# Sending 2 KB per partition of the pooled output on ScalarE's queue beside the loads (3-D average pooling)

## Chip, cores, metric

One Trainium2 chip, one of its cores. The metric is the device time of one execution in microseconds, as the median of several runs. A ratio is the mean time of one kernel's fast runs over the mean of the other's fast runs of the same rounds; it is therefore not quite the ratio of the medians quoted beside it.

## The reference

Average pooling with a 2 x 2 x 2 window over a float32 tensor of 8 x 32 x 32 x 32 x 32 (33.55 MB in, 4.19 MB out).

```python
window = x[:, :, d_s:d_s + 2, h_s:h_s + 2, w_s:w_s + 2]
result[:, :, i, j, k] = np.mean(window, axis=(-3, -2, -1))
```

## The kernel before

Batch and channels make 256 rows, two tiles of 128 partitions. A row has 32768 input values, loaded in units of up to 32 KB per partition (4 MB), five buffers deep, all on SyncE's queue. Per unit VectorE (DVE) adds planes, then neighbours in a row, then neighbouring rows with a scale of 1/8, into a buffer that holds the whole output of one tile (16 KB per partition).

```python
KF = 256
pool_in = ctx.enter_context(tc.tile_pool(name="pin", bufs=5))
obuf = [pool_out.tile([P, 16 * KF], F32, name=f"obuf{t}") for t in range(2)]

plan = [
    (0, 0, (32,)), (0, 32, (32,)), (0, 64, (32,)), (0, 96, (32,)),
    (1, 0, (32,)), (1, 32, (32,)), (1, 64, (16, 16)), (1, 96, (16, 16)),
]                                   # layout of the list changed here
# ... pool_unit: two nc.vector.tensor_add and one tensor_tensor_reduce ...

for t, k0, parts in plan:
    # ... one nc.sync.dma_start per part, then pool_unit per part ...

for t, k0, kb in [(0, 0, 16), (1, 0, 14), (1, 14, 2)]:
    nc.sync.dma_start(
        out=ov[t * P:(t + 1) * P, k0 * KF:(k0 + kb) * KF],
        in_=obuf[t][:, k0 * KF:(k0 + kb) * KF],
    )
# ... at the end of the program SyncE waits for the stores' semaphores ...
```

So there are three stores: the whole first output tile (16 KB per partition, 2 MB), 14 KB and then 2 KB per partition of the second. The 2 KB store covers the last pooled unit, the 14 KB store all of the second tile ahead of it.

Of the kernel before, what the change touches and what calls it, by code (L numbers as in the profile page):

```python
# [1 line left out]

# [4 lines left out]

F32 = mybir.dt.float32
KF = 256


@with_exitstack
def pool_rows(
    ctx: ExitStack,
    tc: tile.TileContext,
    x: bass.AP,
    kernel_size: int,
    out: bass.AP,
):
    nc = tc.nc  # L20
    assert kernel_size == 2, "only kernel_size == 2 supported"

    B, C, D, H, W = x.shape
    P = nc.NUM_PARTITIONS
    assert (B * C, D, H, W) == (2 * P, 32, 32, 32)
    add = mybir.AluOpType.add



    xv = x.rearrange("b c d h w -> (b c) (d h w)")  # L30
    ov = out.rearrange("b c d h w -> (b c) (d h w)")




    pool_in = ctx.enter_context(tc.tile_pool(name="pin", bufs=5))
    pool_out = ctx.enter_context(tc.tile_pool(name="pout", bufs=1))
    obuf = [pool_out.tile([P, 16 * KF], F32, name=f"obuf{t}") for t in range(2)]
    dummy = pool_out.tile([P, 1], F32, name="dummy")


    plan = [
        (0, 0, (32,)),
        (0, 32, (32,)),
        (0, 64, (32,)),
        (0, 96, (32,)),
        (1, 0, (32,)),
        (1, 32, (32,)),
        (1, 64, (16, 16)),
        (1, 96, (16, 16)),  # L50
    ]

    def pool_unit(buf, t, k0, kb):

        od = kb // 8
        a = buf.rearrange("p (o dd e) -> p o dd e", o=od, dd=2)
        b = buf[:, :od * 1024]
        nc.vector.tensor_add(  # L58
            out=b.rearrange("p (o e) -> p o e", o=od), in0=a[:, :, 0], in1=a[:, :, 1])
        bv = b.rearrange("p (e ww) -> p e ww", ww=2)  # L60
        c = buf[:, od * 1024:od * 1536]
        nc.vector.tensor_add(out=c, in0=bv[:, :, 0], in1=bv[:, :, 1])  # L62
        cv = c.rearrange("p (j hh k) -> p j hh k", hh=2, k=16)
        o0 = k0 * KF // 8
        nc.vector.tensor_tensor_reduce(  # L65
            out=obuf[t][:, o0:o0 + od * 256].rearrange("p (j k) -> p j k", k=16),
            in0=cv[:, :, 0], in1=cv[:, :, 1],
            scale=0.125, scalar=0.0, op0=add, op1=add, accum_out=dummy[:, :],
        )

    for t, k0, parts in plan:
        tin = pool_in.tile([P, 32 * KF], F32, tag="tin", name="tin")
        views = []
        o = 0
        for kb in parts:
            v = tin[:, o * KF:(o + kb) * KF]
            nc.sync.dma_start(
                out=v, in_=xv[t * P:(t + 1) * P, (k0 + o) * KF:(k0 + o + kb) * KF])
            views.append((v, k0 + o, kb))
            o += kb  # L80
        for v, k, kb in views:
            pool_unit(v, t, k, kb)


    for t, k0, kb in [(0, 0, 16), (1, 0, 14), (1, 14, 2)]:
        nc.sync.dma_start(
            out=ov[t * P:(t + 1) * P, k0 * KF:(k0 + kb) * KF],
            in_=obuf[t][:, k0 * KF:(k0 + kb) * KF],
        )


def kernel(tc: tile.TileContext, x: bass.AP, kernel_size: int, out: bass.AP):
    nc = tc.nc
    pool_rows(tc, x, kernel_size, out)
    tc.close()
    tc.compile()  # L96
    blocks = nc.main_func.blocks



    opening, program = blocks[0].instructions, blocks[tc.starting_block_idx].instructions
    load = next(i for i in program if isinstance(i, mybir.InstDMACopy))
    assert load.engine == nc.sync.engine
    barrier = next(
        n for n, i in enumerate(opening)
        if i.engine == load.engine and isinstance(i, mybir.InstDrain))
    program.remove(load)
    opening.insert(barrier, load)




    closing = blocks[-1].instructions
    stores = [
        i for i in program
        if isinstance(i, mybir.InstDMACopy) and "out_" in i.outs[0].memref]
    kept = [u.id for i in stores for u in i.sync_info.on_update]
    final = next(
        i for i in closing
        if i.engine == nc.sync.engine and isinstance(i, mybir.InstDrain))  # L120
    waits = {w.id: w for w in final.sync_info.on_wait}
    closing[closing.index(final)] = mybir.InstDrain(
        name=final.name, engine=final.engine, ins=[], outs=[], is_reset_sema=False,
        sync_info=mybir.SyncInfo(
            on_wait=[w for n, w in waits.items() if n not in kept], on_update=[]))


    reset = next(
        n for n, i in enumerate(closing)
        if isinstance(i, mybir.InstDrain) and i.is_reset_sema)  # L130
    first, stop = closing[reset].reset_range_start, closing[reset].reset_range_stop
    assert isinstance(closing[reset + 1], mybir.InstISA)
    while len(closing) > reset:
        closing.pop()
    n = first
    while n < stop:
        m = n
        while m < stop and m not in kept:
            m += 1
        if m > n:  # L140
            closing.append(mybir.InstDrain(
                name=nc.get_next_instruction_name(), engine=nc.gpsimd.engine, ins=[], outs=[],
                is_reset_sema=True, reset_range_start=n, reset_range_stop=m))
            nc.gpsimd.sem_clear(range(n, m))
        n = m + 1
    for n in kept:
        w = waits[n]
        closing.append(mybir.InstEventSemaphore(
            name=nc.get_next_instruction_name(), engine=nc.sync.engine, ins=[], outs=[],
            sync_info=mybir.SyncInfo(  # L150
                on_wait=[w],
                on_update=[mybir.SyncUpdate(
                    sync_type="semaphore", id=n, ant_name=w.ant_name,
                    update_mode="sem-sub-imm", update_value=w.wait_value)])))


# [1 line left out]
_INS = ['x', 'kernel_size']  # L158
_OUTS = [((8, 32, 16, 16, 16), 'float32')]

_NUMBERS = {'kernel_size': 2}


# [26 lines left out]
```

## Time and profile before

| | before |
|---|---|
| time, median of 3 (range) | 91.97 us (91.76 to 92.02) |
| span of the profile (first to last instruction that it counts) | 86.4 us |
| DVE busy | 64.0 us |
| share of the 16 DMA engines on SyncE's queue | 99.2% |
| last store issued, landed | 85.2 us, 90.6 us |

The span ends at DVE's last instruction, while the last stores are still under way: here the span is not the time. Most of the lines that carry the reading stand in the prediction; one more, from the timeline, is VectorE's start after its sixth load:

```profile
60.65 4.43 DVE L58 TENSOR_TENSOR tin<-tin 128x4096 f32<-128x4096 f32 x1 [1.70 <-DMA tin<-in_x_dram]
```

Each record of a DMA packet in the trace has a start, a duration and a size; where the text speaks of packet records, the numbers were worked out from those.

### The profile page before, as it was taken

What the parts mean: (1) busy time and instruction counts of PE and PEld (TensorE: products, weight loads), DVE (VectorE), ACT (ScalarE), POOL (GpSimd) and SP (SyncE); (2) the same over time, 40 slices, a digit from 0 to 9 for tenths busy, and PEclk for the clock granted to TensorE, in tenths of its full rate; (3) what the DMA queues carried; (4) which work ended last, traced back from release to release, by engine and by line L of the source; (5) the groups of instructions that cost most, each with busy time, mean ns of one, the idle gap of its engine ahead of it and who ended that gap; (6) DMA issues with size and microseconds to landing.
All of it is one profiled execution on the core that took longest, in us unless ns stands there. A gap on an engine that the chain in (4) does not pass through costs nothing.

```text
span 86.4 us, 90 instructions
## 1 busy us (share of the span) xinstructions
DVE 64.0 (74%) x40; POOL 0.2 (0%) x4
## 2 busy tenths in 40 slices
DVE  0000039993999749993999749992999999999994
POOL 0000000000000000000000000000000000000000
DMA  8979997999979999799979999799999999998999
GB/s 243 425 319 470 486 470 319 425 486 486 455 319 440 486 486 410 319 486 486 470 319 425 486 486 440 304 470 387 455 402 455 395 455 410 440 425 319 448 432 408
DMA packets 1634, 36.37 MB, mean 421 GB/s; under 512 B 176, under 2 KB 176, under 8 KB 176
## 3 DMA queue, kind: packets, MB, share of 16 engines
q1 hardware_dynamic: 1634, 36.37, 99.2%
HBM read 33.55 MB, written 4.19 MB: 437 GB/s over the span
## 4 chain that ended last, share of the span: by engine, by line
DMA 61%; DVE 37%; issue 0%; DVEq 0%
DMA tin<-in_x_dram 61%; DVE tin L58 21%; DVE tin L62 11%; DVE obuf L65 6%; DVE dummy L65 0%; DVEq L96 0%
## 5 line engine op out<-in xcount | busy, mean ns | idle before, releaser
L58 DVE TENSOR_TENSOR tin<-tin 128x4096 f32<-128x4096 f32 (+1 forms) x10 | 35.7, 3569 | 20.6 <-DMA tin<-in_x_dram 20.6
L62 DVE TENSOR_TENSOR tin<-tin 128x2048 f32<-128x2048 f32 (+1 forms) x10 | 18.6, 1864 | 0.3
L65 DVE CUSTOM_DVE_ANT_1 obuf<-tin 128x1024 f32<-128x1024 f32 (+1 forms) x10 | 10.1, 1011 | 0.3
L65 DVE DVE_READ_ACCUMULATOR2_ANT dummy<- 128x1 f32 x10 | 0.8, 82 | 0.0
L171 POOL MEMSET const-bfloat16-1.0<- 128x1 bf16 x1 | 0.1, 102 | 0.0
L171 POOL MEMSET const-uint8-127<- 128x1 uint8 x1 | 0.1, 101 | 0.0
L171 POOL MEMSET const-float32-1.0<- 128x1 f32 x1 | 0.1, 99 | 0.0
L171 POOL MEMSET const-float32-0.0<- 128x1 f32 x1 | 0.1, 98 | 0.2 <-issue 0.2
## 6 DMA issues: line engine op xcount, KB each, us to landing
tin<-in_x_dram SPq DMA_DIRECT2D x6, 4096.0 KB, 34.9
tin<-in_x_dram SPq DMA_DIRECT2D x4, 2048.0 KB, 38.0
out_dram<-obuf SPq DMA_DIRECT2D x1, 2048.0 KB, 36.4
out_dram<-obuf SPq DMA_DIRECT2D x1, 1792.0 KB, 9.1
out_dram<-obuf SPq DMA_DIRECT2D x1, 256.0 KB, 5.4
```

The costliest lines, as they stand in the source:

```text
L58: nc.vector.tensor_add(out=b.rearrange("p (o e) -> p o e", o=od), in0=a[:, :, 0], in1=a[:, :, 1])
L62: nc.vector.tensor_add(out=c, in0=bv[:, :, 0], in1=bv[:, :, 1])
L65: nc.vector.tensor_tensor_reduce(out=obuf[t][:, o0:o0 + od * 256].rearrange("p (j k) -> p j k", k=16), in0=cv[:, :, 0], in1=cv[:, :, 1], s ...
L171: nc = _bacc.Bacc("TRN2", target_bir_lowering=False, num_devices=1)
```

## The change

The intent, as far as the code shows it: part of the output should leave while the loads run, so that fewer bytes are left for the tail.

```diff
--- before
+++ after
-    for t, k0, kb in [(0, 0, 16), (1, 0, 14), (1, 14, 2)]:
-        nc.sync.dma_start(
+    for queue, t, k0, kb in [
+        (nc.scalar, 0, 0, 2),
+        (nc.sync, 0, 2, 14),
+        (nc.sync, 1, 0, 14),
+        (nc.sync, 1, 14, 2),
+    ]:
+        queue.dma_start(
             out=ov[t * P:(t + 1) * P, k0 * KF:(k0 + kb) * KF],
             in_=obuf[t][:, k0 * KF:(k0 + kb) * KF],
         )
@@
     kept = [u.id for i in stores for u in i.sync_info.on_update]
+    kept = [n for j, n in enumerate(kept) if n not in kept[j + 1:]]
```

The second part keeps one entry per semaphore in the end-of-program list, since two stores may now share one.

## The prediction

> **What bounds the kernel now**
>
> I read the page first (the slices, the queue, the chain), then the windows view by stage, the list of DMA issues, the waits of both engines, and the timeline of the tail.
>
> ```profile
> span 86.4 us, 90 instructions
> ...
> DMA  8979997999979999799979999799999999998999
> ...
> q1 hardware_dynamic: 1634, 36.37, 99.2%
> HBM read 33.55 MB, written 4.19 MB: 437 GB/s over the span
> ...
> DMA 61%; DVE 37%; issue 0%; DVEq 0%
> ```
>
> The reader is to see that one queue (q1, SyncE's) holds all 16 DMA engines for 99.2% of the span. The chain of waits says DMA 61% and DVE 37%, which looks like two bounds in turn. It isn't quite: the chain ends at the last instruction that counts as busy, and the last stores come after it.
>
> The row of slices seems to have holes (the sevens, and GB/s figures of 319). I take them for a counting effect: the trace's packet records show the 16 engines in step, each with one 32 KB packet of 1.213 us (median) after another, so that a short slice catches one more or one fewer start. Put into one chain per engine by their starts and ends, the records leave no gap above 0.11 us from the first packet to the last. Longer windows are flat:
>
> ```profile
> core 0: us, DVE busy (x) POOL busy (x), PEclk, DMA share, GB/s
> 0.00:12.10 12.10, 0.00 (x0) 0.20 (x4) 1.00 0.95 390
> 12.10:60.60 48.50, 39.75 (x20) 0.00 (x0) 1.00 1.00 430
> 60.60:81.00 20.40, 20.14 (x17) 0.00 (x0) 1.00 1.00 415
> 81.00:85.20 4.20, 4.13 (x6) 0.00 (x0) 1.00 1.00 426
> 85.20:90.60 5.40, 0.01 (x1) 0.00 (x0) 1.00 0.83 351
> ```
>
> The DMA share column is 1.00 from 12.1 us to 85.2 us, and 0.83 in the last stretch only because the transfers end inside it. DVE is full only from 60.6 us on. So what sets the end is bytes through the engines: 33.55 + 4.19 = 37.74 MB at 430 GB/s is 87.8 us, and the rest is start-up.
>
> ```profile
> out_dram<-obuf SPq DMA_DIRECT2D x1, 2048.0 KB, 36.4
> out_dram<-obuf SPq DMA_DIRECT2D x1, 1792.0 KB, 9.1
> out_dram<-obuf SPq DMA_DIRECT2D x1, 256.0 KB, 5.4
> ```
>
> The last column is time from issue to landing. A 256 KB store would need 0.61 us at 430 GB/s, yet takes 5.4: it stands in line behind other bytes. The 2 MB store is issued at 49.3 us and lands 36.4 us later, at 85.7: on the same queue as the loads it waits until all of them are through.
>
> ```profile
> 80.93 2.28 DVE L58 TENSOR_TENSOR tin<-tin 128x2048 f32<-128x2048 f32 x1
> 83.25 1.22 DVE L62 TENSOR_TENSOR tin<-tin 128x1024 f32<-128x1024 f32 x1
> 84.50 0.69 DVE L65 CUSTOM_DVE_ANT_1 obuf<-tin 128x512 f32<-128x512 f32 x1
> 85.12 0.08 DVE L65 DVE_READ_ACCUMULATOR2_ANT dummy<- 128x1 f32 x1
> ```
>
> The last unit is pooled at 85.2 us, its store is issued there and lands at 85.2 + 5.4 = 90.6. By the packet records the engines still work on the 1792 KB store until 88.9 to 89.6 and reach the last store only then, so DVE could end some time later at no cost. The measured 91.97 is 1.4 us after that landing; I keep 1.4 as a constant.
>
> ```profile
> DVE tin L58 <- DMA tin<-in_x_dram: 20.6, 6, 12.1
> ```
>
> DVE's only waits are the first six loads. After the sixth, at 60.65, it never waits again.
>
> **What the Trainium skill says**
>
> All four are from its page "DMA: Bandwidth & Descriptors". Section "Issuing engines are not separate DMA queues": DMAs from ScalarE, SyncE and GpSimd run on the same 16 engines and interleave, and a second issuing engine saves issue time only. The trace has nothing to save there: a store's issue takes 0.33 to 0.35 us of SyncE, and SyncE is mostly idle. Section "Where 436 GB/s comes from": a ceiling of 435 GB/s for the 16 ports; the trace agrees, with 430 over 48.5 us. Section "Queues, rings and completion order": each DMA engine goes round robin, packet by packet, over the rings that have work. The kernel before has one ring with data, so its trace cannot show it. Section "Latency and other measured facts", row on HBM row pitch: copies between HBM tensors over the sync and scalar queues ran at 207 to 214 GB/s per direction at their best. I read that as loads and stores in flight together at some 428 GB/s in sum, that is neither a free second direction nor a heavy price for mixing. No trace here shows it yet.
>
> **The change part by part**
>
> 1. Removed: an eighth of the 2048 KB store (256 KB; 2 KB of 16 KB per partition). Each engine owns 8 partitions, so its eight 16 KB packets of 0.611 us become eight of 14 KB. The 1792 KB store already has that size: 0.535 us. Saved at the tail: 8 x (0.611 - 0.535) = 0.61 us per engine.
>
> 2. Added: one store on ScalarE's queue, eight 2 KB packets per engine. The last store has that shape now: 0.084 us each, and 0.009 us for the completion write. Sum 8 x 0.084 + 0.009 = 0.68 us per engine. ScalarE has no other work, so its issue costs nothing on the path. Its data are ready when the first unit is pooled, 20.1 us; the framework may add a wait on an older semaphore, but any moment in the load phase gives the same sum.
>
> 3. Balance on the engines: 0.68 - 0.61 = +0.07 us. No byte goes away, none moves into an idle gap, for there is none.
>
> 4. Moved: the loads. With one small packet between two load packets, the 256 KB are through some 8 x 1.3 = 10 us after they start, so from the fourth load on everything lands 0.68 us later. DVE follows, since it waits for the loads until 60.65: that start becomes 61.3, the 20 us of work behind it is unchanged, and the last unit ends at 85.2 + 0.68 = 85.9. The last load (landing at 80.8 by the records) comes at 81.5, when DVE gets to it at 81.7; still no wait.
>
> 5. Is the later DVE end hidden? The loads free the engines at about 80.7 instead of 80.0, the shorter first store runs to about 84.9, the 1792 KB store to about 89.0. The last store is issued at 85.9; the first load took 1.0 to 1.95 us from issue to its first packet on the various engines, so its packets are ready at 87.9 at the latest, 1 us before the first engine is free. Hidden, with 1 us in hand. The end stays put: 90.6 + 0.07 + 1.4 = 92.0 to 92.1.
>
> So the change exchanges tail time for load time one to one.
>
> **The rivals**
>
> A. The two directions overlap. If the limit is the SBUF write side, the store (which reads SBUF) could pass beside loads for nothing. Then 0.68 us vanishes from the load phase and 0.61 stays saved: 91.97 - 0.61 = about 91.4. For it: the loads' 27.0 GB/s per engine might be a port's rate, not an engine's. Against: stores have the same rate (16 KB in 0.611 us against 0.613 for a 16 KB load packet), and the skill's 207 to 214 per direction.
>
> B. Mixing directions costs. For it: all 16 engines slow down together between 77 and 79.5 us, where 16 KB packets take up to 1.18 us instead of 0.613, some 0.6 us lost per engine, shortly before the first store packet starts at 79.8 to 80.5. If that is the price of turning from loads to stores, eight small packets between loads may pay part of it several times: one more such loss makes 92.6, the full price eight times makes 4.8 us, about 97. Against: it is seen once, 1 to 2 us before the turn itself, so it may be something else, and single small packets need not stop the stream.
>
> C. DVE or the last store becomes the bound. If the early store delayed the loads by over 0.68 + 1 us, the last store's packets would come to idle engines, and further delay would count in full. This needs B first.
>
> D. The turn's loss at 77 us goes away because writes have already happened once: up to 0.6 us less, 91.4 as well. I have nothing for it beyond the position of that loss.
>
> **Range and chances**
>
> The main line gives 92.04. A or D, together some 22%, would give about 91.4; B in a mild form (15%) about 92.6. The weighted middle stays at 92.0, and the three runs before scatter from 91.76 to 92.02. I predict 92.0 us, with 91.3 to 92.7 to hold it 8 times in 10. Faster by over 2% needs 90.1 or less: even the whole moved store for nothing and the whole loss at 77 us removed give 91.97 - 0.61 - 0.6 = 90.8. So 0.02. Slower by over 2% needs 93.8, a strong form of B: 0.05. Within 2%: 0.93.
>
> **What would show it right or wrong**
>
> - In the list of DMA queues a second queue with 0.26 MB, the DMA share still 1.00 in the long windows: right. A share below 1 or a rate clearly under 430 between 20 and 35 us: B. A rate above 435 there: A.
> - The sixth load's wait ending at 61.3 (+0.68): step 4. At 60.65: A.
> - DVE's last instruction at 85.9, so that the span grows by 0.7 us while the measured time does not: steps 4 and 5. A reader of the span alone would call the kernel slower.
> - The time from issue to landing of the last store down from 5.4 to about 4.8, as it is issued later and lands at the same moment: step 5.
> - A time of 91.5 or less makes the one-to-one exchange wrong, one of 92.8 or more the price of mixing.

## The result, and the profile after

The changed kernel: 92.06 us, median of 6 (91.84 to 92.11), against 91.93 (91.76 to 92.09) for the kernel before. The ratio is 1.001, with a 95% interval of 0.9992 to 1.0028: the same time. The prediction's 92.0 holds.

The page of the changed kernel, its span and its queues (packets, MB, share of 16 engines' span):

```profile
span 86.9 us, 90 instructions
...
q1 hardware_dynamic: 1654, 36.39, 98.7%
q10 hardware_dynamic: 144, 0.26, 0.8%
HBM read 33.55 MB, written 4.19 MB: 434 GB/s over the span
```

The second queue is there, with the 0.26 MB, and it has taken its share from the first: 98.7 + 0.8 is 99.5%, where one queue had 99.2%. The bytes are the same. The span is 0.5 us longer although the time isn't, which the prediction had warned of.

The windows by stage, the same as of before:

```profile
core 0: us, DVE busy (x) POOL busy (x), PEclk, DMA share, GB/s
0.00:12.10 12.10, 0.01 (x1) 0.20 (x4) 1.00 0.96 390
12.10:60.60 48.50, 39.74 (x20) 0.00 (x0) 1.00 1.00 429
60.60:81.00 20.40, 19.56 (x15) 0.00 (x0) 1.00 1.00 419
81.00:85.20 4.20, 4.13 (x5) 0.00 (x0) 1.00 1.01 434
85.20:90.60 5.40, 0.60 (x2) 0.00 (x0) 1.00 0.81 341
```

DMA share and GB/s have hardly moved in the long stages (429 for 430, 419 for 415); in the two short ones at the end the rates are 434 for 426 and 341 for 351. What has moved is DVE: 0.60 us of its work now lies in the last stretch, where there was 0.01.

The list of DMA issues (the last number is us from issue to landing, a median where there are two), DVE's waits, and three lines of the timeline:

```profile
out_dram<-obuf SPq DMA_DIRECT2D x2, 1792.0 KB, 22.0
out_dram<-obuf ACTq DMA_DIRECT2D x1, 256.0 KB, 14.1
out_dram<-obuf SPq DMA_DIRECT2D x1, 256.0 KB, 4.6
```

```profile
DVE tin L58 <- DMA tin<-in_x_dram: 21.1, 6, 12.1
```

```profile
20.14 0.38 ACTq L92 DMA_DIRECT2D out_dram<-obuf  x1
...
61.23 4.43 DVE L58 TENSOR_TENSOR tin<-tin 128x4096 f32<-128x4096 f32 x1 [1.69 <-DMA tin<-in_x_dram]
...
85.72 0.08 DVE L65 DVE_READ_ACCUMULATOR2_ANT dummy<- 128x1 f32 x1
```

The early store is issued at 20.14 us, at once when the first unit is pooled. DVE waits 21.1 us for loads where it waited 20.6, its sixth load comes at 61.23 instead of 60.65, and its last instruction starts at 85.72 instead of 85.12. The last store is issued 0.6 us later (85.83 for 85.23) and needs 4.6 us where it needed 5.4: it waits less in line. By the packet records the early store's packets of 0.084 us stand between load packets of 1.213 us, 1.29 us from one to the next on an engine, from 23.5 to 32.6 us.

### The profile page after: what moved, and what is told of

It reads as the page before. It is cut to its first block, busy times and chain, and to the rows that moved or that the text cites. A ratio compares the mean times of both kernels' runs of the same rounds, so it can differ in the third digit from the quotient of the medians.

```text
span 86.9 us, 90 instructions
## 1 busy us (share of the span) xinstructions
DVE 64.0 (74%) x40; POOL 0.2 (0%) x4
## 3 DMA queue, kind: packets, MB, share of 16 engines
q1 hardware_dynamic: 1654, 36.39, 98.7%
## 4 chain that ended last, share of the span: by engine, by line
DMA 61%; DVE 37%; issue 0%; DVEq 0%
DMA tin<-in_x_dram 61%; DVE tin L58 20%; DVE tin L62 11%; DVE obuf L65 6%; DVE dummy L65 0%; DVEq L102 0%
## 5 line engine op out<-in xcount | busy, mean ns | idle before, releaser
L58 DVE TENSOR_TENSOR tin<-tin 128x4096 f32<-128x4096 f32 (+1 forms) x10 | 35.7, 3570 | 21.1 <-DMA tin<-in_x_dram 21.1
## 6 DMA issues: line engine op xcount, KB each, us to landing
out_dram<-obuf ACTq DMA_DIRECT2D x1, 256.0 KB, 14.1
```

The source lines that it names most:

```text
L58: nc.vector.tensor_add(out=b.rearrange("p (o e) -> p o e", o=od), in0=a[:, :, 0], in1=a[:, :, 1])
```

## The experiments

My theory: all 16 engines are busy from the first load to the last store, so time is bytes at a fixed rate, and a store that leaves earlier delays the loads by as much as it shortens the tail. This holds until DVE is so late that a last store comes to idle engines. Rivals: the two directions overlap (a gain), mixing costs (a loss), and the second queue or the cut costs what the early leaving gains. A side question was the stretch of slow packets at 77 to 79 us.

In the diffs below only the list of stores is shown. Runs 1, 4, 5, 10 and 11 are written as edits of the changed kernel or of one another, runs 2, 3, 6 and 7 as edits of the kernel before.

**1. The cut without the early leaving**

```diff
-        (nc.scalar, 0, 0, 2),
+        (nc.sync, 0, 0, 2),
```

> The same four stores as the change, all on SyncE's queue: the cut without the early leaving. One-to-one theory: the tail pays for the cut alone (8 packets of 0.611 us become 8 of 0.535 and 8 of 0.084, and one completion write): +0.07 us, about 92.0, ratio 1.001, as the change itself; DVE ends at 85.2 us again, span 86.4. Rival (the early leaving gained something that the cut cost, or the reverse): ratio differs from the change's 1.001 by more than 0.003.

Measured: 91.91 us (91.61 to 92.3), ratio 0.9989 (0.9966 to 1.0013). DVE's waits, and from the timeline its start after the sixth load:

```profile
DVE tin L58 <- DMA tin<-in_x_dram: 20.5, 6, 12.1
```

```profile
60.63 4.43 DVE L58 TENSOR_TENSOR tin<-tin 128x4096 f32<-128x4096 f32 x1 [1.69 <-DMA tin<-in_x_dram]
```

DVE is back where it was before (60.63 for 60.65, span 86.3), and the time is the same. So the later DVE of the changed kernel comes from the early leaving and not from the cut, and neither is worth anything that can be measured. The two ratios, 0.9989 here and 1.001 of the change, differ by 0.002, within the bound that was set.

**2 and 3. 1 MB more, beside the loads or behind them**

Both keep the stores of before and write half of the first output tile once more into a spare tensor.

```diff
+    spare = nc.dram_tensor("spare", (P, 8 * KF), F32, kind="Internal").ap()
+    nc.scalar.dma_start(out=spare[:, :], in_=obuf[0][:, :8 * KF])   # run 2
+    nc.sync.dma_start(out=spare[:, :], in_=obuf[0][:, :8 * KF])     # run 3
```

> The kernel before with 1 MB more (8 KB per partition, once more the output's first half of the first tile) stored by ScalarE's queue into a spare tensor beside the loads. One-to-one: 8 packets of about 0.306 us more per engine, +2.46 us, 94.4, ratio 1.027; DVE ends at about 87.6. Overlapping directions (rival A): +0 to 0.5, ratio under 1.006. Price for mixing (rival B): more than +3 us, ratio above 1.033, and more than the same bytes cost behind the loads.

> The same 1 MB more, on SyncE's queue behind the loads, so that no store is beside a load. All theories: +2.46 us, 94.4, ratio 1.027, DVE ends at 85.2 as before. The difference from the run with the extra store beside the loads is what mixing itself costs (one-to-one: 0, within 0.3 us).

Measured: 94.23 us (ratio 1.0241, 1.0223 to 1.0259) beside the loads, 94.35 us (1.0257, 1.0237 to 1.0277) behind them. The page's queues and DVE's waits of the run beside the loads, then the same two of the run behind them:

```profile
q1 hardware_dynamic: 1651, 36.61, 96.6%
q10 hardware_dynamic: 144, 1.05, 2.8%
```

```profile
DVE tin L58 <- DMA tin<-in_x_dram: 23.5, 6, 12.3
```

```profile
q1 hardware_dynamic: 1692, 36.37, 99.5%
```

```profile
DVE tin L58 <- DMA tin<-in_x_dram: 20.6, 6, 12.1
```

Beside the loads, the extra megabyte adds 2.9 us to DVE's waiting; behind them, nothing. The time grows by 2.2 us in the one case and 2.3 in the other. This decides between the theories: overlap would have made run 2 about 92, a price for mixing would have made it longer than run 3. In packets of 8 KB, a byte stored beside loads costs what a byte stored behind them costs, within the noise. This is an equality of sums: by the packet records run 2 has slow packets worth 0.49 us per engine beside the loads and 0.05 at the end, run 3 has 0.01 and 0.73 (the table under runs 8 to 10). Both times are a little below the 2.46 us expected.

**4, 5 and 11. How much can leave early?**

The whole, half, and three quarters of the first output tile go on ScalarE's queue in stores of 4 KB per partition, each when its unit is pooled.

```diff
-        (nc.scalar, 0, 0, 2),
-        (nc.sync, 0, 2, 14),
+        (nc.scalar, 0, 0, 4),
+        (nc.scalar, 0, 4, 4),
+        (nc.scalar, 0, 8, 4),      # runs 4 and 11
+        (nc.scalar, 0, 12, 4),     # run 4
+        (nc.sync, 0, 8, 8),        # run 5
+        (nc.sync, 0, 12, 4),       # run 11
```

> The whole first output tile (2 MB) leaves on ScalarE's queue in four stores of 4 KB per partition, each when its unit is pooled. If the early bytes were a gain (rivals A, D): under 91.5. If they are exchanged one to one and nothing else bound: 92.2 (32 packets of 0.16 us for 8 of 0.611). With the limit that I named (the hidden delay of DVE is 1 to 2 us, here it is 5): loads end 5 us later, DVE's last unit ends at about 90.1, its store's packets come to idle engines at 91 to 92, the engines stand still for about 2 us between loads and stores: 94.3, from 93.6 to 95, ratio about 1.026. The slow packets at 77 to 79 us, if they belong to the turn from loads to stores, move to about 82 to 84; if to a moment of the run, they stay.

> Half of the first output tile (1 MB, two stores of 4 KB per partition) leaves on ScalarE's queue, the other half behind the loads. One-to-one with the hidden limit: loads end about 2.5 us later, DVE's last unit at about 87.7, the 1792 KB store is issued at about 83.5 and its first packets are there at 84.4 (0.85 us after issue, as in the run with the whole tile early), just before the engines come free at 85.0: no idle gap, and the time stays at 92.0 (91.7 to 92.4), ratio 1.000 within 0.003; a first idle gap of up to 0.5 us would be the edge of the hiding. If the 0.5 us of slow packets are paid once, with the first stores of 4 KB packets or more, they come at 23 to 30 us with 0.2 us in sum and are gone from the turn at 82 us: then 91.7. If they belong to the turn from loads to stores, 0.5 us of them stay, at about 80 us.

> Three quarters of the first output tile early (three stores of 4 KB per partition), one quarter behind the loads. Between the half (no idle gap, 91.7) and the whole (1.9 us of idle engines, 93.57). Loads end about 3.8 us later than before, the quarter behind them takes 1.3 us and is through at about 84.8; DVE's next to last unit ends at about 84.7, its store's first packets are there at 85.6: an idle gap of 0.5 to 0.8 us, 92.2 to 92.5, ratio 1.002 to 1.006. If the hiding has no such edge (one-to-one alone): 91.7 to 92.0 and no gap.

| early part of the first tile | time (us) | ratio (95% interval) | 1792 KB store issued | idle per engine, 78 to 89 us |
|---|---|---|---|---|
| 2 KB of 16 (the change) | 92.06 | 1.001 (0.9992 to 1.0028) | 81.63 | 0.0 us |
| 8 KB (run 5) | 91.67 | 0.9976 (0.9958 to 0.9994) | 83.55 | 0.0 us |
| 12 KB (run 11) | 92.53 | 1.0054 (1.0038 to 1.007) | 84.89 | 0.9 us |
| 16 KB (run 4) | 93.57 | 1.0171 (1.0151 to 1.0191) | 85.79 | 2.2 us |

The last column is worked out from the packet records: the time in which no packet runs, averaged over the 16 engines. The windows view of 84.7 to 86.6 us shows the same, for 8, 12 and 16 KB in this order:

```profile
84.70:86.60 1.90, 1.86 (x2) 0.00 (x0) 1.00 1.01 430
```

```profile
84.70:86.60 1.90, 1.90 (x3) 0.00 (x0) 1.00 0.63 265
```

```profile
84.70:86.60 1.90, 1.86 (x4) 0.00 (x0) 1.00 0.00 0
```

The next to last number is the DMA share: full, two thirds, nothing. With the whole tile early there is nothing left to do between the loads (through at 84.7 us) and the 1792 KB store, whose data are pooled at 85.8 and whose first packet starts at 86.6. So the later DVE is hidden only while some earlier output is still waiting to be sent behind the loads. The change, at 0.6 us of delay, is far from that edge; half a tile (2.5 us) is just inside it, three quarters are outside. The margin of half a tile is about 0.1 us by an estimate from the records: its 1792 KB store is issued at 83.55 us, 0.85 us later (the time that run 4 shows) is 84.4, and the first engine comes free at 84.5.

Run 5 (91.67) came out just under the range of 91.7 to 92.4, with its ratio inside; of the two readings of the slow packets, neither came true as a whole (0.18 us of them early, 0.26 left at the end; see runs 8 to 10). Run 4 came out below the range that I had given (93.57 against 93.6 to 95). I had taken 1 to 2 us from a store's issue to its packets on an idle engine, as for the first load. It was 0.85 us (issued at 85.79, first packet at 86.64), and the last store landed 2.1 us after its issue. Run 11 met its ratio and just missed its upper bound in microseconds (92.53 against 92.5).

**6 and 7. The cut in four behind the loads; the stores in the other order**

```diff
-        (0, 0, 16), (1, 0, 14), (1, 14, 2)
+        (0, 0, 4), (0, 4, 4), (0, 8, 4), (0, 12, 4), (1, 0, 14), (1, 14, 2)     # run 6
+        (1, 0, 14), (0, 0, 16), (1, 14, 2)                                      # run 7
```

> The first output tile in four stores of 4 KB per partition, all on SyncE's queue behind the loads: the cut of the run with the whole tile early, without the early leaving. Bytes and cut alone: 32 packets of 0.159 us for 8 of 0.611, +0.2 us, 92.2, ratio 1.002; DVE ends at 85.2. The difference from the run with the whole tile early (93.57) is then the idle gap there and not the cut. Slow packets: if large store packets make them, less than the 0.54 us of before; if the turn does, 0.5 us as before at 77 to 79.

> Before with the two large stores of SyncE's queue in the other order, so that no store waits behind the loads: the first one is issued at 81.0, when the next to last unit is pooled. Engines idle from about 80 to 81.9, the stores (9.8 us) run to 91.7, time about 93.6 (93.2 to 94), ratio 1.018: an early enough stored tile is what keeps the engines fed between loads and last stores. Slow packets at 77 to 79: if the end of the loads or a moment of the run makes them, they stay; if a store queued right behind the loads does, they are gone (the time is the same either way, since DVE sets the issue).

Measured: run 6 took 92.01 us (ratio 1.0008, 0.9986 to 1.0029), so the cut isn't what made run 4 slow. Run 7 took 93.71 us (1.0203, 1.0176 to 1.023), as expected. The window of 80 to 82 us, first of the kernel before, then of run 7:

```profile
80.00:82.00 2.00, 1.97 (x4) 0.00 (x0) 1.00 0.98 418
```

```profile
80.00:82.00 2.00, 1.97 (x4) 0.00 (x0) 1.00 0.00 0
```

DVE does the same work in both; in run 7 no engine moves a byte for 2 us (by the packet records from 80.3 to 82.4 us), since SyncE's queue holds back the finished first tile behind a store whose data aren't pooled yet. The profiled execution of run 7 was its longest (94.29 us; the other three lie at 93.64 to 93.75) and had slow packets scattered over the load phase, so I use it mainly for the gap. For the slow packets it shows two things, in this one odd profile: 0.04 us at 76 to 84 us, where the engines stand idle behind the loads, and 0.33 us at 20 to 45 us, although no store is in flight there.

**8, 9 and 10. Is the gain of run 5 real, and what is it?**

Run 8 is the changed kernel and run 9 is run 5, unaltered; run 10 sends the same half in packets of 2 KB:

```diff
-        (nc.scalar, 0, 0, 4),
-        (nc.scalar, 0, 4, 4),
+        (nc.scalar, 0, 0, 2),
+        (nc.scalar, 0, 2, 2),
+        (nc.scalar, 0, 4, 2),
+        (nc.scalar, 0, 6, 2),
```

> The changed kernel once more, beside the run with half the tile early: 92.0 us, ratio 1.000 to 1.002, slow packets of about 0.45 us per engine at 77 to 79 us.

> The run with half of the first output tile early, once more, since its gain (ratio 0.9976) is near the noise. If the gain is real: 91.7, ratio 0.996 to 0.999, under the changed kernel of the same rounds by 0.2 to 0.4 us. If it was chance: 92.0.

> The same half early, in four stores of 2 KB per partition, the packet size of the change. Packets: 32 of 0.084 for 16 of 0.159, +0.14 us against the run in 4 KB pieces. If the amount sent early is what relieves the turn from loads to stores, the slow packets there are at most 0.24 us as with the 4 KB pieces and none show at 23 to 45 us: 91.6 to 91.9. If only larger early packets relieve it, 0.45 us stay at about 80 us: 92.1.

Measured in the same rounds: 92.02 us for the changed kernel (ratio to before 0.9993, 0.9976 to 1.0011), 91.71 for half in 4 KB (0.9969, 0.995 to 0.9988), 91.99 for half in 2 KB (0.9992, 0.9977 to 1.0007). So the version with half of the tile early, in two stores of 4 KB per partition, beat the kernel before in both sets of rounds and the changed kernel in the one set that they shared, by about 0.3 us or 0.3%. It is the best version here, and still "the same" by a measure of 2%. Its executions fall in two groups in both runs: four of six lie at 91.61 to 91.71 us, two at 91.94 to 92.04. Both of its profiles are from the faster group.

Where the 0.3 us are from I could see only in part. The packet records give, per engine, the time by which packets ran over the usual time of their size:

| | slow packets at 76 to 84 us | slow packets at 20 to 45 us |
|---|---|---|
| before | 0.54 us | 0.00 |
| the change; again (run 8) | 0.45; 0.54 | 0.01; 0.05 |
| cut alone (run 1) | 0.59 | 0.02 |
| 1 MB more behind the loads (run 3) | 0.73 | 0.01 |
| cut in four (run 6) | 0.44 | 0.01 |
| half early in 2 KB (run 10) | 0.50 | 0.06 |
| half early in 4 KB (runs 5; 9) | 0.26; 0.07 | 0.18; 0.33 |
| three quarters early in 4 KB (run 11) | 0.27 | 0.19 |
| 1 MB more beside the loads, 8 KB packets (run 2) | 0.05 | 0.49 |
| whole tile early in 4 KB (run 4), idle engines before the stores | 0.00 | 0.23 |

Wherever stores stand right behind the loads, and only packets of 2 KB or none have gone out before, about half a microsecond is lost there. Where packets of 4 or 8 KB have gone out among the loads, less is lost at the end, and something is lost earlier. That the early stores cause the earlier loss is not shown: run 7 has 0.33 us there without any. The amount sent early is not what counts: the same half in 2 KB packets kept its 0.5 us, which speaks against the first reading in the expectation of run 10. Of the 0.28 us between the medians of runs 9 and 10, another 0.14 is the price of the larger number of packets, worked out in that expectation. For run 5 and run 9 the sum of both columns (0.44 and 0.40 us) is 0.10 and 0.14 below that of before, less than half of the gain. Counted from 20 us to the end, with the packets that the table leaves out, the loss is 0.67 us before, 0.46 and 0.47 in runs 5 and 9, and 0.58 in run 10, but 0.53 and 0.86 in the two profiles of the change: two profiles of one kernel differ by as much as the gain, so the records can't assign it. What makes these packets slow is not settled, and each row is one profiled execution, two where two values stand.

## Why the prediction was right

- **What bounds the kernel.** Right: bytes through 16 full engines. Runs 2 and 3 show it by its price: 1 MB more costs 2.2 or 2.3 us wherever it goes.
- **Steps 1 to 3, the balance of +0.07 us.** In size below what 6 runs can tell. The sum is not contradicted, and no more: the measured difference is 0.13 us of medians, with an interval that holds both 0 and 0.07. Run 1 shows that the cut by itself is not measurable.
- **Step 4, the loads 0.68 us later.** The mechanism is right, the size a little too large: the sixth load came 0.58 us later, DVE's end 0.60. The delay was there from the third load on (DVE starts on it at 32.08 us for 31.50), one load sooner than forecast. On an engine a store packet put the next one 1.29 us behind, 0.077 more than a load packet alone, where I had taken the 0.084 that such packets take one behind another. The early store also needed 3.4 us from its issue to its first packet and landed after 14.1; I had given 10 us for the draining and nothing for the start.
- **Step 5, the later DVE end is hidden.** Right: 4.6 us from issue to landing (predicted 4.8), and the packet records show no idle engine. The margin of 1 us was taken too small. Half a tile early delays DVE by 2.5 us at no cost, because a store reaches idle engines 0.85 us after its issue and not after up to 1.95.
- **Rival A, overlap.** Refuted by run 2. What the prediction took from the skill's row on copies between HBM tensors was about another kind of transfer, which no run here made; its reading as loads and stores side by side is not tested. **Rival B, a price for mixing.** Refuted as a sum by runs 2 and 3, which differ by 0.1 us with overlapping intervals. The slow packets that had suggested it are real and do sit at the turn from loads to stores: they are gone where engines stand idle in between (run 4, and run 7 in its one profile, where nothing was sent early). Their cause is open.
- **Rival C, a last store as bound.** Real, but not for this change: it needs three quarters of a tile early (run 11). And the store that meets idle engines first is the 1792 KB one, not the last, as the prediction had it.
- **Rival D, writes that have already happened take the loss away.** Not for 2 KB packets (runs 8 and 10). For larger early packets the loss at the end does shrink, but slow packets stand earlier as well (0.18 to 0.49 us), and which causes which is open.
- **The signs that were named.** The second queue, the full share, the later DVE, the longer span at equal time and the shorter landing of the last store all came. One sign was badly chosen: a rate under 430 between 20 and 35 us was to speak for rival B. That window gives 424 GB/s after and 439 before; but the window of 35 to 60 us gives 439 after and 427 before, and both together 433 and 431. Even 15 us are short enough for the counting effect of packets in step.

## What to carry to other kernels

When the DMA engines are full from the first load to the last store, moving a store earlier, or to another queue, mostly moves time (here the best version gained 0.3 of 92 us): look for idle engines first, and only then for a better order. What is worth keeping is some finished output behind the last load, so that the engines have work while the last units are computed. Judge by the measured time, since a span that ends with the last compute instruction can grow while the time stands still.

## What the Trainium skill lacked or had wrong

- "DMA: Bandwidth & Descriptors", section "Issuing engines are not separate DMA queues": confirmed (the early store's packets stand between load packets, 1.29 us from one to the next on an engine, and a store on ScalarE's queue and the same cut on SyncE's take 92.06 and 91.91 us, both the same as before). It lacks what the interleaving costs: 1 MB stored beside loads adds 2.2 us, behind loads 2.3.
- The same page, section "Where 436 GB/s comes from", says that for transfers between HBM and SBUF the HBM side (about 358 GB/s) binds. For a core alone that is wrong: this one held 430 GB/s over 48.5 us of loads. The page's own single-core measurements are near this; the sentence lacks the condition that the page gives there, both cores of a pair streaming, which no run here tries.
- The same page, section "Latency and other measured facts": it gives about 600 ns to the first byte, and no figure for a store that comes on an empty queue beside full engines. Here it was 3.4 us from issue to first packet beside loads (the change), against 0.85 us on idle engines (run 4).
- "Perfetto Trace Analysis", section "DMA Optimizations", says that batching small transfers, from 2 KB to 4 or 8 KB, can improve throughput dramatically. It speaks of whole transfers, and none here is under 256 KB, so that is not tested; it lacks what packet sizes inside a large transfer are worth. Here the gap is small: back to back, packets of 2 KB took 0.084 us (24.4 GB/s per engine) and packets of 32 KB 1.213 us (27.0): 10%.
- No page has the slow stretch of about 0.5 us per engine when stores stand right behind loads on a queue (16 KB packets up to 1.18 us instead of 0.613).
